# A two-layer decoder trunk on one Trainium2 core: both attentions' value projections by the seven-product form

## Chip, cores, metric

The program runs on one core of one Trainium2 chip. The metric is the device time of one execution in microseconds; the time before is the median of three runs.

A core has five engines that run side by side, each through its own list of instructions in a fixed order: PE (matmuls and transposes; PEld is its weight load), DVE (element by element arithmetic), ACT (copies, casts, activations), POOL, and SP, which here issues the weight loads. They wait for each other by semaphores. PE writes its sums to PSUM banks of 128 x 512 floats, from which DVE and ACT read.

## What is computed

Two layers; each is a token mixer, a cross-attention over 256 memory rows and a squared-ReLU MLP, all on 256 tokens of width 2048. The part that is changed is `v` below, in both layers:

```python
def memory_attention(h, mem_n, w_q, w_kv, w_o):
    q = (h @ w_q).reshape(bsz, seq, X_HEADS, X_HEAD_DIM)
    k, v = jnp.split(mem_n @ w_kv, 2, axis=-1)
    ...
    scores = jnp.einsum('bshd,bmhd->bhsm', q, k).astype(F32) * (X_HEAD_DIM ** -0.5)
    p = jax.nn.softmax(scores, axis=-1).astype(v.dtype)
    o = jnp.einsum('bhsm,bmhd->bshd', p, v).reshape(bsz, seq, X_HEADS * X_HEAD_DIM)
    return o @ w_o
```

`mem_n` is the memory after an RMS norm with a weight of its own in each layer; there are 4 heads of 512.

## The kernel before

**Precision.** Every float32 operand of a large product is split in two: `hi` is the value cast to fp32r by ACT, `lo` the rest, subtracted by DVE (`split`, L101 and L102). A product of 128 rows by 512 columns is then three matmuls: hi·hi, hi·lo, lo·hi. A weight tile of 256 rows by 512 columns (512 KB) is loaded by SP into `wraw` (4 buffers), split into `whi` and `wlo` (3 buffers each), and with two halves of the tokens, `t`, it feeds 12 matmuls. All operands of a layer's width lie in `act` tiles: 16 row tiles `kt`, hi and lo.

**An attention** (`attention`). `mem_prep` prepares the memory's rows in four pieces: POOL loads a chunk (`memc`, 2 buffers), and `scale_chunk` scales it by the norm's weight, hi on ACT (L232) and lo on DVE (L233). The pieces are side work: `tick`, called once for each weight tile, takes one and puts its instructions in with a lower priority. Then, head by head, `proj` makes q and k (`gemm_feat`, L163 and L165), and `softmax` the probabilities, transposed and split, `pTh` and `pTl`.

Then come the values, head by head: `gemm_tok` with `wv` (8 weight tiles, 96 matmuls, L145 to L147), the scaling by the row's norm into `vh` (ACT, L505) and `vl` (DVE, L506), 24 matmuls for the weighted sum over the memory's rows (L516, 256 columns each), and the split of that into `oT`. Head 0's output also goes through `token_sums`: four sums and differences of its row tiles and halves (L614 to L617) and their split, which the next product needs.

**The seven-product form** (`gemm_seven`). The output projection `wo` and most of the last MLP's down projection take two column tiles `n0` and `n0+1` at once. For the first four row tiles they form a 2 x 2 by 2 x 2 block product with seven products instead of eight: the left sums come from `token_sums`, the right ones are made from the four loaded weight tiles `ws` (L687, L693, L698, L703, into `run` or in place). Each product is a split and 6 matmuls; parts that belong to several outputs are copied out of PSUM by ACT (`kept`, L679) and added by DVE. The rest of the row tiles go the plain way (`direct`), between the products. At the end `gather` adds what is in the banks to the residual.

**Order.** The program is written in this order; a scheduler then lays each engine's list out, by priority and by its own estimate of when an operand is ready. Buffers come from pools with tags: tiles with one tag share its slots (2 in the attention's pool) and get them in the written order.

Of the kernel before, what the change touches and what calls it, by code (L numbers as in the profile page):

```python
# [16 lines left out]
P = 128  # L17
D = 2048
S = 256
# [19 lines left out]
class Trunk:  # L39
# [230 lines left out]
    def mem_prep(self, pool, layer):  # L270

        act = self.new_act()

        def piece(j):
            m = pool.tile([P, 4, S], F32, name="memc")
            self.nc.gpsimd.dma_start(out=m, in_=self.a["mem_t"][j])
            self.scale_chunk(m, 4 + layer, act, j)

        self.side += [lambda j=j: piece(j) for j in range(NCH)]
        return act  # L280


# [152 lines left out]
    def attention(self, x, layer, cur, nxt):  # L435
# [3 lines left out]
        with tc.tile_pool(name="at", bufs=2, reuse_waits="tile") as ap:  # L439
            qs = ap.tile([P, 2], F32, name="qs", bufs=1)  # L440
            nqs = ap.tile([P, 2], F32, name="nqs", bufs=1)
            pTs = []
            memT = self.mem_prep(ap, layer)

            def proj(act, w, n, nm):
                h = ap.tile([P, 4, S], F32R, name=nm + "h")
                l = ap.tile([P, 4, S], F32R, name=nm + "l")
                for i in range(2):
                    z = ap.tile([P, 2, S], F32, name="z")
                    self.gemm_feat(act, w, 2 * n + i, z)  # L450
                    self.split(h[:, 2 * i:2 * i + 2], l[:, 2 * i:2 * i + 2], z)
                return h, l

            def softmax(q, k, hd):
                sc = self.ps([P, 2, S])
                for t in range(2):
                    sl = slice(t * P, (t + 1) * P)
                    for f in range(4):
                        mm = lambda s, m, b, e: nc.tensor.matmul(  # L459
                            sc[:, t, :], s, m, start=b, stop=e, skip_group_check=True)  # L460
                        mm(q[0][:, f, sl], k[0][:, f, :], f == 0 and t == 0, False)
                        mm(q[0][:, f, sl], k[1][:, f, :], False, False)
# [12 lines left out]
                nc.vector.reciprocal(out=rs, in_=sm)  # L475
                for t in range(2):
                    nc.vector.tensor_scalar(out=e[:, t, :], in0=e[:, t, :], scalar1=rs[:, t:t + 1],
                                            scalar2=None, op0=ALU.mult)
                pt = self.ps([P, 2, S])
                for m in range(2):  # L480
                    for t in range(2):
                        nc.tensor.transpose(pt[:, m, t * P:(t + 1) * P], e[:, t, m * P:(m + 1) * P], self.ident)
                ph = ap.tile([P, 2, S], F32R, name="pTh", bufs=4)
                pl = ap.tile([P, 2, S], F32R, name="pTl", bufs=4)
                self.split(ph, pl, pt)
                pTs.append((ph, pl))

            for hd in range(HEADS):
                q = proj(hT, wq, hd, "q")
                self.flush()  # L490
                k = proj(memT, wk, hd, "k")
                if hd == 0:
                    rstd = cur.rstd()
                    nc.vector.tensor_scalar(out=qs, in0=rstd, scalar1=QSCALE, scalar2=None, op0=ALU.mult)
                    nc.vector.tensor_scalar(out=nqs, in0=rstd, scalar1=-QSCALE, scalar2=None, op0=ALU.mult)
                softmax(q, k, hd)

            oT = self.new_act()
            for hd in range(HEADS):
                acc = self.gemm_tok(memT, wv, hd)  # L500
                vh = ap.tile([P, 2, HD], F32R, name="vh")
                vl = ap.tile([P, 2, HD], F32R, name="vl")
                for t in range(2):
                    r = self.rstd_mem[:, t:t + 1]
                    nc.scalar.activation(out=vh[:, t, :], in_=acc[:, t, :], func=AF.Copy, scale=r)  # L505
                    nc.vector.scalar_tensor_tensor(out=vl[:, t, :], in0=acc[:, t, :], scalar=r,  # L506
                                                   in1=vh[:, t, :].bitcast(F32), op0=ALU.mult, op1=ALU.subtract)
                ph, pl = pTs[hd]
                ops = [self.ps([P, 2, S]) for _ in range(2)]
                for fp in range(2):  # L510
                    op = ops[fp]
                    for k in range(2):
                        f = 2 * fp + k
                        sl = slice(f * P, (f + 1) * P)
                        for m in range(2):
                            mm = lambda s, mv, b, e: nc.tensor.matmul(  # L516
                                op[:, k, :], s, mv, start=b, stop=e, skip_group_check=True)
                            mm(vh[:, m, sl], ph[:, m, :], k == 0 and m == 0, False)
                            mm(vh[:, m, sl], pl[:, m, :], False, False)
                            mm(vl[:, m, sl], ph[:, m, :], False, m == 1)  # L520
                    kt = 4 * hd + 2 * fp
                    self.split(oT[0][:, kt:kt + 2, :], oT[1][:, kt:kt + 2, :], op)
                if hd == 0:
                    for fp in range(2):
                        o = ap.tile([P, 2, S], F32, name="o", tag="e")
                        nc.scalar.copy(out=o, in_=ops[fp])
                        ops[fp] = o
                    sums = self.token_sums(ap.tile([P, KB * NB], F32, name="s", tag="qh"),
                                           lambda: ap.tile([P, 4, 2, P], F32R, name="sums", tag="kh"), *ops)

            nxt.start()
            count = iter(range(100))
            ws = lambda: ap.tile([P, KB * NB], F32, name="ws", tag=("ql", "qh")[next(count) % 2])
            run = lambda: ap.tile([P, KB * NB], F32, name="run", tag="kl")
            pair = {}

            def kept(i):
                if i in (1, 2):
                    return ap.tile([P, NB], F32, name="kept", tag="z")
                if i == 0:  # L540
                    pair[0] = ap.tile([P, 2, NB], F32, name="kept2", tag="kl")
                return pair[0][:, i // 3, :]

            def gather(t, n, part):
                xc = x[:, t, n * NB:(n + 1) * NB]
                nc.vector.tensor_tensor(out=xc, in0=part, in1=xc, op=ALU.add)

            for j in range(0, NCH, 2):
                self.gemm_seven((ws, run, kept), lambda kt, t: [f[:, kt, t * P:(t + 1) * P] for f in oT[:2]],
                                sums, wo, j, 0, gather)  # L550
                for n in (j, j + 1):
                    self.at(1 + n - j, lambda n=n: nxt.chunk(x, n))


    def mlp(self, x, layer, cur, nxt):
# [3 lines left out]
        with tc.tile_pool(name="ml", bufs=4, reuse_waits="tile") as mp:  # L559
# [5 lines left out]
            for b in range(DFF // D):  # L565
# [25 lines left out]
                for n in range(NCH):  # L591
                    end = b == DFF // D - 1
                    if nxt.closing and not (end and n >= NCH - 2):
                        if n % 2 == 0:
                            self.gemm_seven((ws, run, kept), lambda kt, t: [f[:, kt % 4, t * P:(t + 1) * P]
                                                                            for f in hid[kt // 4]],
                                            sums, wd, n, b * KT, gather)
                    elif nxt.closing and end and n == NCH - 1:
                        self.gemm_last(hid, wd, n, b * KT, lambda t, acc: (gather(t, n, acc), nxt.finish(x, t)))
                        break  # L600
# [18 lines left out]
        self.split(sh, sl, s)  # L619
        return sh, sl  # L620

    def gemm_seven(self, tiles, token, sums, w, n0, k0, gather):

# [90 lines left out]
        for keys in (((1, 0), (0, 1)), ((0, 0), (1, 1))):  # L714
            for e in ends:
                next(e)
            for t, j in keys:
                gather(t, n0 + j, banks[t, j])
        for e in ends:
            next(e, None)  # L720

# [648 lines left out]
```

## Time and profile before

| | us |
|---|---|
| median of 3 runs (2842.48 to 2843.86) | 2843.06 |
| the profiled execution, whole | 2844.99 |
| its span, first to last instruction | 2843.3 |

The profile is of one execution. Its page gives the busy time of each engine, the granted clock of PE (here 0.997 on the mean), the chain of work that ended last, and groups of instructions by line, engine, operation and tile. A timeline row is start, length, engine, line, operation, output and input; a bracket behind it is the idle time of the engine just ahead, and what ended it. Neighbouring instructions of one engine overlap a little: a matmul of 512 columns has a length of 0.39 us, though the next one begins earlier.

### The profile page before, as it was taken

What the parts mean: (1) busy time and instruction counts of PE and PEld (TensorE: products, weight loads), DVE (VectorE), ACT (ScalarE), POOL (GpSimd) and SP (SyncE); (2) the same over time, 40 slices, a digit from 0 to 9 for tenths busy, and PEclk for the clock granted to TensorE, in tenths of its full rate; (3) what the DMA queues carried; (4) which work ended last, traced back from release to release, by engine and by line L of the source; (5) the groups of instructions that cost most, each with busy time, mean ns of one, the idle gap of its engine ahead of it and who ended that gap; (6) DMA issues with size and microseconds to landing.
All of it is one profiled execution on the core that took longest, in us unless ns stands there. A gap on an engine that the chain in (4) does not pass through costs nothing.

```text
span 2843.3 us, 39689 instructions
## 1 busy us (share of the span) xinstructions
PE 2803.5 (99%) x15172; PEld 2347.3 (83%) x15172; DVE 1959.4 (69%) x2707; ACT 1394.7 (49%) x1801; POOL 204.8 (7%) x380
## 2 busy tenths in 40 slices
PE   8999999999999999999999999999999999999998
PEld 6888888888888888888787788888888888888886
DVE  6765655578878878787567666555677767667665
ACT  5445544454544444444455445444554545445453
POOL 1000000001022222222001000000000000000000
PEclk9999999999999999999999999999999999999999
DMA  8766665657677777776879766566556565565655
GB/s 282 212 202 207 194 179 185 183 163 230 191 221 219 218 224 222 216 223 207 231 240 296 220 203 209 181 182 195 166 181 213 166 217 188 167 218 162 223 159 155
DMA packets 180463, 579.55 MB, mean 204 GB/s; under 512 B 37440, under 2 KB 39664, under 8 KB 179504
## 3 DMA queue, kind: packets, MB, share of 16 engines
q1 hardware_dynamic: 141440, 511.77, 57.8%
q0 software_dynamic: 38688, 65.19, 8.5%
q8 instruction: 118, 1.93, 0.3%
q14 instruction: 73, 0.60, 0.1%
q10 hardware_dynamic: 144, 0.07, 0.0%
HBM read 553.88 MB, written 22.94 MB: 203 GB/s over the span
## 4 chain that ended last, share of the span: by engine, by line
PE 90%; DVE 4%; DMA 3%; ACT 1%; issue 1%; POOL 0%; SPq 0%; DVEq 0%; ACTq 0%; POOLq 0%
PE acc L163 24%; PE acc L650 15%; PE acc L165 13%; PE acc L146 7%; PE acc L147 7%; PE acc L145 7%; PE acc L735 4%; PE acc L734 4%; PE acc L733 4%; DVE wlo L102 1%; PE ps L516 1%; PE ps L459 1%; ACT whi L101 1%; PE ps L214 1%; DMA wraw<-in_f_w_down 1%
## 5 line engine op out<-in xcount | busy, mean ns | idle before, releaser
L102 DVE TENSOR_TENSOR wlo<-wraw,whi 128x1024 fp32r<-128x1024 f32 x908 | 1109.2, 1223 | 672.0 <-ACT whi L101 668.0
L101 ACT CAST whi<-wraw 128x1024 fp32r<-128x1024 f32 x908 | 954.9, 1052 | 1133.7 <-PE acc L163 374.4
L163 PE MATMUL acc<-act,whi 128*128 128x512 f32 x3072 | 1084.5, 397 | 0.5 <-ACT whi L101 0.4
L165 PE MATMUL acc<-act,wlo 128*128 128x256 f32 x3072 | 864.7, 281 | 1.3 <-DVE wlo L102 1.3
L163 PEld LDWEIGHTS acc<-act,whi 128*128 128x128 f32 x3072 | 576.3, 188 | 135.3 <-issue 1.6
L165 PEld LDWEIGHTS acc<-act,wlo 128*128 128x128 f32 x3072 | 580.2, 189 | 6.0 <-DVE wlo L102 2.2
L145 PE MATMUL acc<-whi,act 128*128 128x512 f32 x992 | 391.1, 394 | 8.7 <-ACT whi L101 7.3
L146 PE MATMUL acc<-wlo,act 128*128 128x512 f32 x992 | 389.2, 392 | 6.2 <-DVE wlo L102 6.2
L147 PE MATMUL acc<-whi,act 128*128 128x512 f32 x992 | 388.5, 392 | 0.3 <-DVE act L102 0.3
L145 PEld LDWEIGHTS acc<-whi,act 128*128 128x128 f32 x992 | 187.1, 189 | 49.4 <-ACT whi L101 8.6
L146 PEld LDWEIGHTS acc<-wlo,act 128*128 128x128 f32 x992 | 187.3, 189 | 46.1 <-DVE wlo L102 8.6
L147 PEld LDWEIGHTS acc<-whi,act 128*128 128x128 f32 x992 | 187.3, 189 | 38.6 <-DVE act L102 0.7
L734 PE MATMUL acc<-wlo,hh 128*128 128x512 f32 x544 | 215.5, 396 | 0.8 <-DVE wlo L102 0.8
L733 PE MATMUL acc<-whi,hh 128*128 128x512 f32 x544 | 215.1, 395 | 0.0
L735 PE MATMUL acc<-whi,hl 128*128 128x512 f32 x544 | 214.7, 395 | 0.0
L650 PE MATMUL acc<-wlo,hh 128*128 128x512 f32 x378 | 147.6, 390 | 1.6 <-DVE wlo L102 1.6
L650 PE MATMUL acc<-whi,hh 128*128 128x512 f32 x378 | 147.6, 391 | 0.5
L650 PE MATMUL acc<-whi,hl 128*128 128x512 f32 x378 | 147.2, 389 | 0.0
L650 PE MATMUL acc<-whi,act 128*128 128x512 f32 x432 | 135.8, 389 | 0.0
L734 PEld LDWEIGHTS acc<-wlo,hh 128*128 128x128 f32 x544 | 102.5, 188 | 24.5 <-DVE wlo L102 1.8
L735 PEld LDWEIGHTS acc<-whi,hl 128*128 128x128 f32 x544 | 102.5, 188 | 22.8 <-issue 1.6
L733 PEld LDWEIGHTS acc<-whi,hh 128*128 128x128 f32 x544 | 102.6, 189 | 22.5 <-issue 0.4
(325 smaller groups left out, 2726.1 us busy)
## 6 DMA issues: line engine op xcount, KB each, us to landing
wraw<-in_f_w_up SPq DMA_DIRECT2D x256, 512.0 KB, 4.2
wraw<-in_f_w_down SPq DMA_DIRECT2D x228, 512.0 KB, 4.3
wraw<-in_a_w_in SPq DMA_DIRECT2D x64, 512.0 KB, 4.4
wraw<-in_x_w_q SPq DMA_DIRECT2D x64, 512.0 KB, 3.7
wraw<-in_x_w_k SPq DMA_DIRECT2D x64, 512.0 KB, 3.7
wraw<-in_x_w_v SPq DMA_DIRECT2D x64, 512.0 KB, 3.6
wraw<-in_b_w_out SPq DMA_DIRECT2D x64, 512.0 KB, 4.5
wraw<-in_x_w_o SPq DMA_DIRECT2D x48, 512.0 KB, 3.8
```

What stands on the lines that cost most here:

```text
L101: self.nc.scalar.copy(out=hi, in_=src)
L102: self.nc.vector.tensor_tensor(out=lo, in0=src, in1=hi.bitcast(F32), op=ALU.subtract)
L145: nc.tensor.matmul(out[t], ah[:, kt, sl], hi[:, kk, :], start=st, stop=False)
L146: nc.tensor.matmul(out[t], ah[:, kt, sl], lo[:, kk, :], start=False, stop=False)
L147: nc.tensor.matmul(out[t], al[:, kt, sl], hi[:, kk, :], start=False, stop=en)
L163: nc.tensor.matmul(acc[:, f, :], hi[:, kk, sl], both[:, kt].rearrange("p a s -> p (a s)"), start=st, stop=False, skip_group_check=True)
L165: nc.tensor.matmul(acc[:, f, 0:S], lo[:, kk, sl], ah[:, kt, :], start=False, stop=en, skip_group_check=True)
L214: nc.tensor.transpose(pt[:, kk, t * P:(t + 1) * P], src[:, t, c:c + P], self.ident)
L650: mm = lambda s, m, e: nc.tensor.matmul(out, s, m, start=key not in begun, stop=e, skip_group_check=True)
L733: nc.tensor.matmul(acc[:, t, :], ah[:, kt % 4, sl], hi[:, kk, :], start=st, stop=False)
L734: nc.tensor.matmul(acc[:, t, :], ah[:, kt % 4, sl], lo[:, kk, :], start=False, stop=False)
L735: nc.tensor.matmul(acc[:, t, :], al[:, kt % 4, sl], hi[:, kk, :], start=False, stop=en)
```

## The change

The value projections also go through `gemm_seven`, two heads at a time. For that

- `mem_prep` takes the pieces in the order 1, 2, 3, 0, and piece 0 is scaled in place by four DVE instructions, split whole (one ACT cast, one DVE subtraction), and put through `token_sums` into `mem_sums`;
- `gemm_seven` takes a second function, `end`, for what is in the banks at its end. In `values` the parts are collected in `more`, added at the end where there is one, and scaled into `vh` and `vl`;
- the weighted sums of both heads (`weighted`) stand behind the pair's product, and head 0's `token_sums` behind its weighted sum, as before;
- the loaded tiles `ws` have a list of homes (slots of the v tiles for heads 0 and 1, then of the q tiles), `run` and `ends` have one fixed slot for the whole stage.

```diff
@@ mem_prep
-            self.scale_chunk(m, 4 + layer, act, j)
-
-        self.side += [lambda j=j: piece(j) for j in range(NCH)]
+            if j:
+                return self.scale_chunk(m, 4 + layer, act, j)
+            for k in range(4):
+                self.nc.vector.tensor_scalar(out=m[:, k, :], in0=m[:, k, :], scalar1=self.gcol[:, 4 + layer, k:k + 1],
+                                             scalar2=None, op0=ALU.mult)
+            self.split(act[0][:, 0:4, :], act[1][:, 0:4, :], m)
+            self.mem_sums = self.token_sums(pool.tile([P, KB * NB], F32, name="s", tag="vh"),
+                                            lambda: pool.tile([P, 4, 2, P], F32R, name="msums", tag="memc"),
+                                            m[:, 0:2], m[:, 2:4])
+
+        self.side += [lambda j=j: piece(j) for j in (1, 2, 3, 0)]
@@ attention
-            for hd in range(HEADS):
-                acc = self.gemm_tok(memT, wv, hd)
...
+            homes = iter(("vh", "vl") * 2 + ("ql", "qh") * 6)
+            ws = lambda: ap.tile([P, KB * NB], F32, name="ws", tag=next(homes))
+            run = ap.tile([P, KB * NB], F32, name="run", tag="kh")
+            ends = ap.tile([P, 2, NB], F32, name="ends", tag="kl")
+            kept = lambda i: ap.tile([P, NB], F32, name="kept", tag="z") if i in (1, 2) else ends[:, i // 3, :]
...
+                def end(t, n, src):
...
+                    part = more.pop((t, n), None)
+                    if part is not None:
+                        nc.vector.tensor_tensor(out=part, in0=src, in1=part, op=ALU.add)
+                        src = part
+                    vh, vl = (f[:, t, :] for f in vs[n - h0])
                     r = self.rstd_mem[:, t:t + 1]
+                    nc.scalar.activation(out=vh, in_=src, func=AF.Copy, scale=r)
+                    nc.vector.scalar_tensor_tensor(out=vl, in0=src, scalar=r, in1=vh.bitcast(F32),
+                                                   op0=ALU.mult, op1=ALU.subtract)
+
+                self.gemm_seven(tiles, token(memT), self.mem_sums, wv, h0, 0,
+                                lambda t, n, part: more.update({(t, n): part}), end)
+                return vs
...
+            for h0 in range(0, HEADS, 2):
+                vs = values(h0)
+                for i in range(2):
+                    ops = weighted(h0 + i, *vs[i])
+                    if h0 + i == 0:
...
+                        sums = self.token_sums(ap.tile([P, KB * NB], F32, name="s", tag="qh"),
+                                               lambda: ap.tile([P, 4, 2, P], F32R, name="sums", tag=next(tags)), *ops)
@@ gemm_seven
-                gather(t, n0 + j, banks[t, j])
+                end(t, n0 + j, banks[t, j])
```

Three places in the engines' lists, all laid out by the scheduler. Line numbers of the changed kernel are other than those of the profile: L675 is the matmul of `gemm_seven` (L650 before), L545 the weighted sum (L516), L529 `vl` (L506), L638 to L641 the sums (L614 to L617), L712 and L718 combinations of weight tiles.

**PE, end of head 0's values in layer 0.** Before; `acc` is head 1's product:

```order
L145 MATMUL acc_4304<-whi_4307,act_2322 128x512
L516 MATMUL ps_4261<-pTh_2827,vh_4255 128x256
L516 MATMUL ps_4261<-pTl_2828,vh_4255 128x256
L516 MATMUL ps_4262<-pTh_2827,vh_4255 128x256
L516 MATMUL ps_4262<-pTl_2828,vh_4255 128x256
L146 MATMUL acc_4304<-wlo_4308,act_2322 128x512
L516 MATMUL ps_4261<-pTh_2827,vl_4256 128x256
L516 MATMUL ps_4262<-pTh_2827,vl_4256 128x256
L147 MATMUL acc_4304<-whi_4307,act_2322 128x512
```

After, the last product of heads 0 and 1 and the first weighted sums (ps_4441 is head 0's, ps_4484 head 1's):

```order
L675 MATMUL acc_4120<-wlo_4405,act_2322 128x512
L675 MATMUL acc_4120<-whi_4404,act_2322 128x512
L545 MATMUL ps_4441<-pTh_2834,vh_4414 128x256
L545 MATMUL ps_4441<-pTl_2835,vh_4414 128x256
L545 MATMUL ps_4442<-pTh_2834,vh_4414 128x256
L545 MATMUL ps_4442<-pTl_2835,vh_4414 128x256
L545 MATMUL ps_4484<-pTh_3260,vh_4416 128x256
```

and the last of the 48 weighted sums and the first product of heads 2 and 3:

```order
L545 MATMUL ps_4485<-pTh_3260,vl_4417 128x256
L545 MATMUL ps_4485<-pTh_3260,vh_4416 128x256
L545 MATMUL ps_4485<-pTl_3261,vh_4416 128x256
L545 MATMUL ps_4485<-pTh_3260,vl_4417 128x256
L675 MATMUL acc_4514<-whi_4525,msums_2480 128x512
L675 MATMUL acc_4514<-wlo_4526,msums_2480 128x512
```

The next head's matmuls were mixed in among the weighted sums; now the 48 stand in one piece, with nothing of the next pair among them. In layer 1 the list is the same.

**DVE, the same place.** Before; `wlo` are head 1's weight splits, `act` is the split of `oT`, `s` and `sums` the row sums for wo:

```order
L102 TENSOR_TENSOR wlo_4326<-wraw_4323,whi_4325 128x1024
L506 SCALAR_TENSOR_TENSOR vl_4256<-acc_4110,rstd_mem_1959,vh_4255 128x512
L102 TENSOR_TENSOR wlo_4344<-wraw_4341,whi_4343 128x1024
L506 SCALAR_TENSOR_TENSOR vl_4256<-acc_4110,rstd_mem_1959,vh_4255 128x512
L102 TENSOR_TENSOR act_4109<-ps_4261,act_4109 128x2x256
L102 TENSOR_TENSOR act_4109<-ps_4262,act_4109 128x2x256
L102 TENSOR_TENSOR wlo_4362<-wraw_4359,whi_4361 128x1024
L614 TENSOR_TENSOR s_4295<-o_4291,o_4293 128x256
```

After, from the last `vl` on (ps_4485 is head 1's second half, `run` and `wlo_4526` the first right-hand sum of heads 2 and 3 and its split):

```order
L529 SCALAR_TENSOR_TENSOR vl_4417<-ends_4118,rstd_mem_1959,vh_4416 128x512
L102 TENSOR_TENSOR act_4116<-ps_4441,act_4116 128x2x256
L102 TENSOR_TENSOR act_4116<-ps_4442,act_4116 128x2x256
L640 TENSOR_TENSOR s_4475<-o_4471 128x256
L102 TENSOR_TENSOR act_4116<-ps_4484,act_4116 128x2x256
L638 TENSOR_TENSOR s_4475<-o_4471,o_4473 128x256
L102 TENSOR_TENSOR act_4116<-ps_4485,act_4116 128x2x256
L639 TENSOR_TENSOR s_4475<-s_4475,o_4471 128x256
L641 TENSOR_TENSOR s_4475<-o_4473,s_4475 128x256
L102 TENSOR_TENSOR sums_4481<-s_4475,sums_4480 128x1024
L712 TENSOR_TENSOR run_4117<-ws_4518,ws_4516 128x1024
L102 TENSOR_TENSOR wlo_4526<-run_4117,whi_4525 128x1024
```

The next product's splits stood ahead of the `oT` splits and the row sums; now they stand behind both.

**DVE, the last piece of the memory's rows in layer 1.** Before, the end of chunk 2, and chunk 3 around a weight split:

```order
L102 TENSOR_TENSOR wlo<-wraw,whi 128x1024
L233 SCALAR_TENSOR_TENSOR act<-memc,gcol,act 128x256 x4
L194 TENSOR_TENSOR rstd<-rstd,rstd_t_16223 128x2
L190 SCALAR_TENSOR_TENSOR rstd_t_16223<-rstd,rs_v 128x1
L102 TENSOR_TENSOR wlo<-wraw,whi 128x1024
L233 SCALAR_TENSOR_TENSOR act<-memc,gcol,act 128x256 x2
```

After, the end of chunk 3, and chunk 0:

```order
L233 SCALAR_TENSOR_TENSOR act<-memc,gcol,act 128x256 x2
L280 TENSOR_SCALAR memc<-memc,gcol 128x256 x4
L102 TENSOR_TENSOR wlo<-wraw,whi 128x1024
L638 TENSOR_TENSOR s<-memc 128x256
L102 TENSOR_TENSOR act<-memc,act 128x4x256
L639 TENSOR_TENSOR s<-s,memc 128x256
```

Chunk 0 stands where chunk 3 stood, its scalings ahead of a weight split, its low part behind that and one of the sums.

More of the change, by code (lines that the diff above doesn't have):

```diff
@@ L498, in attention, with values, weighted @@
             oT = self.new_act()
-            for hd in range(HEADS):
-                acc = self.gemm_tok(memT, wv, hd)
-                vh = ap.tile([P, 2, HD], F32R, name="vh")
-                vl = ap.tile([P, 2, HD], F32R, name="vl")
-                for t in range(2):
-                    r = self.rstd_mem[:, t:t + 1]
-                    nc.scalar.activation(out=vh[:, t, :], in_=acc[:, t, :], func=AF.Copy, scale=r)
-                    nc.vector.scalar_tensor_tensor(out=vl[:, t, :], in0=acc[:, t, :], scalar=r,
-                                                   in1=vh[:, t, :].bitcast(F32), op0=ALU.mult, op1=ALU.subtract)
+            homes = iter(("vh", "vl") * 2 + ("ql", "qh") * 6)
[3 more added lines that the diff above has]
+            kept = lambda i: ap.tile([P, NB], F32, name="kept", tag="z") if i in (1, 2) else ends[:, i // 3, :]
+            tiles = ws, lambda: run, kept
+            token = lambda act: lambda kt, t: [f[:, kt, t * P:(t + 1) * P] for f in act[:2]]
+            def values(h0):
+                vs, more = [], {}
+                def end(t, n, src):
+                    if not vs:
+                        vs.extend([ap.tile([P, 2, HD], F32R, name=nm) for nm in ("vh", "vl")] for _ in range(2))
+                    part = more.pop((t, n), None)
[3 more added lines that the diff above has]
+                    vh, vl = (f[:, t, :] for f in vs[n - h0])
+                    r = self.rstd_mem[:, t:t + 1]
+                    nc.scalar.activation(out=vh, in_=src, func=AF.Copy, scale=r)
[4 more added lines that the diff above has]
+                return vs
+            def weighted(hd, vh, vl):
                 ph, pl = pTs[hd]
@@ L522, in attention @@
                     self.split(oT[0][:, kt:kt + 2, :], oT[1][:, kt:kt + 2, :], op)
[L523 to L529, printed above, removed]
-            nxt.start()
[L532 to L542, printed above, removed]
+                return ops
+            for h0 in range(0, HEADS, 2):
[3 more added lines that the diff above has]
+                    if h0 + i == 0:
+                        for fp in range(2):
+                            o = ap.tile([P, 2, S], F32, name="o", tag="e")
+                            nc.scalar.copy(out=o, in_=ops[fp])
+                            ops[fp] = o
+                        tags = iter(("kh", "kl"))
+                        sums = self.token_sums(ap.tile([P, KB * NB], F32, name="s", tag="qh"),
+                                               lambda: ap.tile([P, 4, 2, P], F32R, name="sums", tag=next(tags)), *ops)
+            nxt.start()
             def gather(t, n, part):
@@ L548, in attention @@
             for j in range(0, NCH, 2):
-                self.gemm_seven((ws, run, kept), lambda kt, t: [f[:, kt, t * P:(t + 1) * P] for f in oT[:2]],
-                                sums, wo, j, 0, gather)
+                self.gemm_seven(tiles, token(oT), sums, wo, j, 0, gather, gather)
                 for n in (j, j + 1):
@@ L596, in mlp @@
                                                                             for f in hid[kt // 4]],
-                                            sums, wd, n, b * KT, gather)
+                                            sums, wd, n, b * KT, gather, gather)
                     elif nxt.closing and end and n == NCH - 1:
@@ L620, in token_sums, with gemm_seven @@
         return sh, sl
-    def gemm_seven(self, tiles, token, sums, w, n0, k0, gather):
+    def gemm_seven(self, tiles, token, sums, w, n0, k0, gather, end):
         nc = self.nc
```

## The prediction

> **What bounds the kernel now.** I read the page from the top: first the busy shares, then the chain of work that ended last, then the waits.
>
> ```profile
> PE 2803.5 (99%) x15172; PEld 2347.3 (83%) x15172; DVE 1959.4 (69%) x2707; ACT 1394.7 (49%) x1801; POOL 204.8 (7%) x380
> PE 90%; DVE 4%; DMA 3%; ACT 1%; issue 1%; POOL 0%; SPq 0%; DVEq 0%; ACTq 0%; POOLq 0%
> ```
>
> PE is busy for 2803.5 of 2843.3 us, so it stands idle for only about 40 us in the whole program, and 90% of the last chain is PE. A matmul less is time saved, and any wait of PE is time lost: nothing later has slack in which it could be won back. Two stretches, layer 0's value projection from a little ahead to a little behind, and a stretch of layer 1's, with the columns PE, PEld, DVE, ACT, POOL, granted clock, DMA share and GB/s:
>
> ```profile
> 467.00:660.00 193.00, 193.00 (x932) 161.06 (x932) 126.70 (x151) 96.20 (x115) 6.07 (x16) 1.00 0.58 178
> 2000.00:2200.00 200.00, 200.00 (x1013) 168.89 (x1012) 138.97 (x164) 105.66 (x137) 2.14 (x4) 1.00 0.60 189
> ```
>
> There PE has no idle time at all, DVE is busy 66% and ACT 50%. So on the sum of work there is room for more on DVE and ACT; whether it is there at the right moment is a question of order. The pitch of the matmuls comes from the timeline of PE:
>
> ```profile
> 1993.51 0.39 PE L145 MATMUL acc<-whi,act 128*128 128x512 f32 x1
> ...
> 1998.95 0.39 PE L145 MATMUL acc<-whi,act 128*128 128x512 f32 x1
> ...
> 2010.31 0.28 PE L516 MATMUL ps<-pTl,vh 128*128 128x256 f32 x1
> 2010.43 0.28 PE L516 MATMUL ps<-pTh,vh 128*128 128x256 f32 x1
> ```
>
> Between the first two lie 24 matmuls of the value projection: 5.44 us, **0.227 us each**; its 0.39 us is a length, of which 0.16 overlaps the next. The weighted sums (L516, 256 columns) go every 0.12 us.
>
> **What it removes.** Each pair of heads has 7 products instead of 8 for the first four row tiles: 6 matmuls less, 24 in the two layers. 24 x 0.227 = **5.4 us**, and this is all that there is to gain.
>
> **What it adds in sum.** For each pair of heads DVE gets three weight splits, four combinations of weight tiles, three additions to kept parts and one sum of kept parts; ACT three splits and four copies. By the rows below that is 7 x 1.22 + 4 x 0.68 = 11.3 us of DVE a pair, 23 a layer: 126.7 + 23 = 150 of 193 us in the first stretch. ACT gets 3 x 1.05 + 4 x 0.59 = 5.5 a pair. By sums this lies beside PE and I cost it at nothing; the weight loads stay 64 of 512 KB. What it costs where the cover is gone are the next two parts.
>
> **The end of heads 0 and 1, in both layers.** Durations (busy sum and mean ns; the last row is a load, us to landing):
>
> ```profile
> L102 DVE TENSOR_TENSOR wlo<-wraw,whi 128x1024 fp32r<-128x1024 f32 x908 | 1109.2, 1223 | 672.0 <-ACT whi L101 668.0 <-PE ps L992 0.2
> L546 DVE TENSOR_TENSOR x<-acc,x 128x512 f32<-128x512 f32 x16 | 10.3, 682 | 0.4 <-PE acc L650 0.4
> L687 DVE TENSOR_TENSOR run<-ws 128x1024 f32<-128x1024 f32 x11 | 13.4, 1221 | 0.1
> L102 DVE TENSOR_TENSOR act<-ps,act 128x512 fp32r<-128x512 f32 x32 | 21.3, 688 | 13.7 <-ACT act L101 12.4
> L102 DVE TENSOR_TENSOR sums<-s,sums 128x1024 fp32r<-128x1024 f32 x2 | 2.5, 1225 | 0.0
> L617 DVE TENSOR_TENSOR s<-o,s 128x256 f32<-128x256 f32 x2 | 0.8, 424 | 0.1
> L679 ACT COPY kept<-acc 128x512 f32<-128x512 f32 x44 | 24.8, 589 | 8.1 <-PE acc L650 8.1
> L505 ACT ACTIVATE vh<-acc,rstd_mem 128x512 fp32r<-128x512 f32 x16 | 11.0, 690 | 13.3 <-PE acc L147 13.3
> L101 ACT CAST act<-ps 128x512 fp32r<-128x512 f32 x32 | 17.9, 586 | 20.0 <-PE ps L516 20.0
> L101 ACT CAST sums<-s 128x1024 fp32r<-128x1024 f32 x2 | 2.1, 1055 | 0.4 <-DVE s L617 0.4
> L101 ACT CAST whi<-run 128x1024 fp32r<-128x1024 f32 x33 | 34.8, 1055 | 29.2 <-PE acc L650 14.5 <-issue 6.1 <-PE acc L163 5.2
> wraw<-in_x_w_v SPq DMA_DIRECT2D x64, 512.0 KB, 3.6
> ```
>
> Before, the order on PE lets the next head's matmuls run between the weighted sums, with their weight splits on DVE ahead of the sums of rows. After, PE has all 48 weighted sums of heads 0 and 1 directly behind the first pair's last product, and the second pair's first product directly behind those; DVE has the first split of the second pair behind the oT splits and behind the sums for wo, which wait for the weighted sums. So the cover is gone on both sides. With T for the moment at which PE could issue on:
>
> - Ahead of the weighted sums: the last product lands at T+0.16, the part is added (0.68), ACT makes vh (0.69): PE goes on at about T+1.6. **Wait 1.6.**
> - Weighted sums: 48 x 0.12 = 5.8, issued by T+7.35, landed at T+7.5. Then in a row: ACT casts the last of oT (0.59), DVE its low part (0.69), two sums (2 x 0.42), ACT casts the sums (1.06), DVE their low part (1.22), the first combination (1.22, beginning some 0.1 early, as neighbours on DVE do), ACT its cast (1.06). With some 0.04 for each of the handovers that is T+14.2; PE has been free since T+7.35. **Wait 6.9.**
> - The second matmul needs the low part (1.22), one matmul of 0.23 lies beside it. **Wait 1.0.**
> - DVE is now at its start with five operations ahead of the next direct tile (two splits, two combinations, its own split; 1.14 apart): 15.4 + 5 x 1.14 = T+21.1, while PE has 17 matmuls, held by their own two splits, and is through at T+19.5. **Wait 1.5.** Later tiles have 12 matmuls (2.7 us) against one or two operations, so it gets back its lead.
>
> Sum 11.0 a layer, **22.0** in both. At the end of heads 2 and 3 the order on PE puts 13 matmuls of wo (3.0 us) ahead of the weighted sums, over the 1.6, and wo goes on behind them with splits that are made: 0, at most the same 1.6 a layer. SP's order: the second loaded tile of the second pair (its slot of tag qh comes behind that of the sums) goes out behind the first pair's last raw tiles; 3.6 us from issue to landing, long before T+12. The fourth waits for the sums' low part (T+12.0), lands at about T+15.6 and is first read by the third of those five operations, at T+17.7: 2 us of slack. Behind it SP holds wo's tiles and the raw tiles from the fifth on; four raw tiles are in the buffers. I cost SP at nothing; a load of double length (3.6 more) would make it 1.6 a layer.
>
> **The rows of the memory.** Chunk 0, which k's first matmul reads, is now prepared last of the four, and in more steps. Layer 1, from the timelines of ACT, DVE and PE, and the price of the new scaling (its nearest row, a scaling by a column):
>
> ```profile
> 1766.29 0.91 ACT L232 ACTIVATE act<-memc,gcol 128x256 fp32r<-128x256 f32 x2 [2.81 <-DMA memc<-in_mem_t]
> 1769.32 0.87 DVE L233 SCALAR_TENSOR_TENSOR act<-memc,gcol,act 128x256 fp32r<-128x256 f32 x2
> 1766.71 0.40 PE L163 MATMUL acc<-act,whi 128*128 128x512 f32 x1
> L477 DVE TENSOR_SCALAR e<-e,rsm 128x256 f32<-128x256 f32 x16 | 4.9, 351 | 0.3
> ```
>
> The fourth piece lands at 1766.25 (ACT stood 2.81 us for it) and is ready at 1770.2. Before, this was chunk 3, the last that k reads; k begins at 1766.71, with chunk 0. Now: four scalings 1.15 us (0.27 apart), to 1767.4; ACT's cast to 1768.5, beside it a weight split and one sum on DVE, to 1768.9; low part (1.22) to 1770.1. PE begins k at about 1770.2: **3.5 us.** Bounds: 3.0, if nothing lay between cast and low part, and 4.7, if the scalings had the 0.44 of the row above each and two more sums went ahead. The sums themselves are needed much later: nothing. Layer 0:
>
> ```profile
> 310.36 1.67 DVE L233 SCALAR_TENSOR_TENSOR act<-memc,gcol,act 128x256 fp32r<-128x256 f32 x4
> 314.90 0.39 PE L163 MATMUL acc<-act,whi 128*128 128x512 f32 x1
> ```
>
> There the piece is in its buffer when DVE comes to it at 310.36: scalings to 311.5, a sum and a split to 313.0, low part to 314.2, ahead of 314.90. Nothing, with 0.7 us to spare.
>
> **The clock after a wait.** One wait of this length is in the trace, between two stages; then the matmuls behind it, and the window's granted clock (the last number but two):
>
> ```profile
> 1383.77 0.33 PE L214 MATMUL ps<-ident,x 128*128 128x128 f32 x1 [2.73 <-DVE x L588]
> ...
> 1386.18 0.63 PE L734 MATMUL acc<-wlo,hh 128*128 128x512 f32 x1
> ...
> 1387.89 0.51 PE L735 MATMUL acc<-whi,hl 128*128 128x512 f32 x1
> 1384.70:1388.10 3.40, 3.40 (x13) 0.50 0.95 368
> ```
>
> After 2.73 us (and 0.33 more) PE ran 3.4 us at half the clock: 4 matmuls in 1.71 us, 0.43 each. That takes 3.4 x (1 - 0.227/0.43) = 1.6 us. So I add 1.6 behind the wait of 3.5. Behind the wait of 6.9 the same is sure to come, but there PE loses 1.0 and 1.5 to DVE anyway, and a slower PE lets DVE catch up: 0.3 a layer, 0.6, between nothing and two such windows (3.2 a layer).
>
> [...]
>
> **Sum.** -5.4 + 22.0 + 0.6 + 3.5 + 1.6 = **+22.3 us**. On the profiled execution (2844.99 us for the span of 2843.3) that is 2867.3; it ran 1.9 above the median, which gives 2843.06 + 22.3 = **2865.4**.
>
> **Rivals.**
>
> - *The stalls are covered.* The matmuls go, and PE finds its splits made, as it does in both stretches above (no idle time). Then -5.4: 2837.6, and not slower. Its mechanism is a DVE that has the second pair's first split done by T+7.35; the price is nothing, and it decides from waits under 2.7 us a layer. For it speaks that DVE has 43 us free in the stretch; against it that the free time lies elsewhere, since each engine keeps its order and the split stands behind the sums. 4 in 100. Since 0.2% (5.7 us, about what a measurement of this kernel can tell from no change) is more than 5.4, even this is no clear gain.
> - *The memory rows are in time.* If the last piece lands 3.5 us sooner, -5.4 + 22.0 + 0.6: 2860.3. For it: the piece of layer 0 was there in time. Against: its load starts when the second piece's buffer is free, as before. 20 in 100.
> - *The clock costs its full price.* Two windows behind each long wait: -5.4 + 22.0 + 6.4 + 3.5 + 3.2 = +29.7, 2872.8. [...] Against: the work behind it waits for DVE anyway. 17 in 100.
> - *It doesn't do what it says*: excluded, the order of PE has 24 matmuls less.
>
> **How the numbers follow.** My forecast, with some us on either side, has 55 in 100; 4 are left for what I don't see (a late load, splits that lag for longer). Faster by over 0.2%: 1 in 100; within 0.2%: 4, the first rival; slower: 95. The range goes from 2856 (the second rival, with 1.5 + 1.5 us less should DVE's last lag be covered in both layers and the clock cost nothing) to 2874 (the third, and a little of SP's 1.6).
>
> **What would show it.** Right: PE waits of 6 to 8 us in both layers, released by ACT at the cast of a combination (whi from run), behind the weighted sums of heads 0 and 1; PE idle at the first weighted sum for some 1.6; PE idle for about 3.5 at k's first matmul in layer 1 and not in layer 0; windows at clock 0.50 behind these. Busy PE time without them falls by some 5 us. Wrong: no such wait in the list of PE's waits, or the splits of the second pair on DVE ahead of the sums; then the first rival holds. If PE waits there for a DMA, my reading of SP is wrong.

## The result and the profile after

The changed kernel takes **2866.42 us** in the median of 5 runs (2864.29 to 2869.78), the kernel before 2842.58 us (2842.48 to 2843.86): a ratio over the rounds of **1.0087, 95% interval 1.0076 to 1.0098** (the two medians alone give 1.0084). The forecast was 2865.4, in a range of 2856 to 2874. The profiled execution took 2864.42 us, with a span of 2862.7 us, 19.4 more than the span before.

First the busy shares and the chain that ended last, on the page of the changed kernel:

```profile
PE 2804.2 (98%) x15148; PEld 2348.5 (82%) x15148; DVE 2003.9 (70%) x2763; ACT 1417.3 (50%) x1825; POOL 204.7 (7%) x380
PE 88%; DVE 5%; DMA 3%; ACT 2%; issue 2%; POOL 0%; SPq 0%; DVEq 0%; ACTq 0%; POOLq 0%
```

PE has 24 matmuls less (15148 against 15172) and is still busy for 0.7 us more. That is a first hint of the clock, since the same matmul is busy for longer at half of it (0.80 us where 0.39 is usual, below). The list of PE's waits (us in total, times, longest) says where the rest went:

```profile
PE acc L675 <- ACT whi L101: 13.6, 2, 6.8
...
PE ps L545 <- ACT vh L528: 3.1, 2, 1.5
PE acc L675 <- DVE wlo L102: 3.1, 6, 0.5
...
PE acc L163 <- DVE act L102: 2.7, 1, 2.7
```

None of the first, second and fourth stood in the list before. There are two long waits, one for each layer, released by ACT's cast; two short ones ahead of the weighted sums (L545); and one at k's first matmul (L163), which is in layer 1 alone. On the timeline the shorter two are these, the first in layer 0:

```profile
527.51 0.39 PE L545 MATMUL ps<-pTh,vh 128*128 128x256 f32 x1 [1.54 <-ACT vh L528]
...
1777.43 0.47 PE L163 MATMUL acc<-act,whi 128*128 128x512 f32 x1 [2.74 <-DVE act L102]
```

The chain behind the long wait in layer 0 is on the timeline of DVE, from the last of the oT splits on:

```profile
534.08 0.69 DVE L102 TENSOR_TENSOR act<-ps,act 128x512 fp32r<-128x512 f32 x1
534.69 0.41 DVE L639 TENSOR_TENSOR s<-s,o 128x256 f32<-128x256 f32 x1
535.14 0.42 DVE L641 TENSOR_TENSOR s<-o,s 128x256 f32<-128x256 f32 x1
536.67 1.22 DVE L102 TENSOR_TENSOR sums<-s,sums 128x1024 fp32r<-128x1024 f32 x1 [1.11 <-ACT sums L101]
537.82 1.22 DVE L712 TENSOR_TENSOR run<-ws 128x1024 f32<-128x1024 f32 x1
540.20 1.22 DVE L102 TENSOR_TENSOR wlo<-run,whi 128x1024 fp32r<-128x1024 f32 x1 [1.16 <-ACT whi L101]
```

and PE beside it, with the last weighted sum of head 1 and the first product of heads 2 and 3:

```profile
533.15 0.28 PE L545 MATMUL ps<-pTh,vl 128*128 128x256 f32 x1
...
540.22 0.80 PE L675 MATMUL acc<-whi,msums 128*128 128x512 f32 x1 [6.79 <-ACT whi L101]
```

From one start to the other it is 7.07 us, of which 0.12 is the matmul's own pitch: 6.95 for the step that the forecast put at 6.9. The sequence on DVE is the one that was predicted, operation by operation. That matmul took 0.80 us where 0.39 is usual, because the granted clock was 0.50 there (first stretch below). Three stretches (columns PE, PEld, DVE, ACT, POOL, granted clock, DMA share, GB/s), behind the long wait of layer 0, behind that of layer 1, and behind k's:

```profile
535.90:546.10 10.20, 5.42 (x12) 3.95 (x13) 8.26 (x8) 4.72 (x5) 0.00 (x0) 0.50 0.35 103
2003.70:2010.50 6.80, 3.61 (x8) 2.53 (x9) 5.63 (x6) 3.22 (x4) 0.00 (x0) 0.50 0.41 97
1778.40:1781.80 3.40, 3.40 (x12) 2.81 (x11) 3.36 (x5) 1.57 (x2) 0.00 (x0) 0.50 0.26 70
```

Half clock lasted 10.2, 6.8 and 3.4 us there: three windows of 3.4 us, two, and one. Part of the first two stretches lies inside the wait itself, where it costs nothing: PE's first product came only at 540.22 in layer 0 and at 2006.42 in layer 1. PE worked for 5.42 and 3.61 us at half clock there. By the two pitches of the forecast, 0.227 and 0.43 us, that is an estimated 2.6 and 1.7 us lost.

### The profile page after: what moved, and what is told of

Its sections match the earlier page's. It is cut to its first block, busy times and chain, and to the rows that moved or that the text cites. A ratio compares the mean times of both kernels' runs of the same rounds, so it can differ in the third digit from the quotient of the medians.

```text
span 2862.7 us, 39726 instructions
## 1 busy us (share of the span) xinstructions
PE 2804.2 (98%) x15148; PEld 2348.5 (82%) x15148; DVE 2003.9 (70%) x2763; ACT 1417.3 (50%) x1825; POOL 204.7 (7%) x380
## 4 chain that ended last, share of the span: by engine, by line
PE 88%; DVE 5%; DMA 3%; ACT 2%; issue 2%; POOL 0%; SPq 0%; DVEq 0%; ACTq 0%; POOLq 0%
PE acc L163 24%; PE acc L675 20%; PE acc L165 12%; PE acc L146 5%; PE acc L145 5%; PE acc L147 5%; PE acc L760 4%; PE acc L759 4%; PE acc L758 4%; DVE wlo L102 2%; ACT whi L101 1%; PE ps L467 1%; DMA wraw<-in_f_w_down 1%; PE ps L545 1%; PE ps L214 1%
## 5 line engine op out<-in xcount | busy, mean ns | idle before, releaser
L102 DVE TENSOR_TENSOR wlo<-wraw,whi 128x1024 fp32r<-128x1024 f32 x892 | 1088.9, 1222 | 643.7 <-ACT whi L101 639.7
L101 ACT CAST whi<-wraw 128x1024 fp32r<-128x1024 f32 x892 | 938.5, 1052 | 1116.7 <-PE acc L163 371.4
L163 PE MATMUL acc<-act,whi 128*128 128x512 f32 x3072 | 1083.9, 396 | 3.3 <-DVE act L102 2.7
L163 PEld LDWEIGHTS acc<-act,whi 128*128 128x128 f32 x3072 | 576.7, 188 | 136.7 <-issue 4.6
L145 PE MATMUL acc<-whi,act 128*128 128x512 f32 x736 | 291.9, 397 | 9.9 <-ACT whi L101 8.4
L146 PE MATMUL acc<-wlo,act 128*128 128x512 f32 x736 | 290.3, 394 | 3.5 <-DVE wlo L102 3.5
L147 PE MATMUL acc<-whi,act 128*128 128x512 f32 x736 | 288.9, 392 | 0.3 <-DVE act L102 0.3
L675 PE MATMUL acc<-whi,act 128*128 128x512 f32 x864 | 273.7, 391 | 0.6 <-DVE ends L524 0.5
L675 PEld LDWEIGHTS acc<-whi,act 128*128 128x128 f32 x864 | 162.9, 189 | 36.1 <-ACT whi L101 1.3
L145 PEld LDWEIGHTS acc<-whi,act 128*128 128x128 f32 x736 | 139.6, 190 | 40.8 <-ACT whi L101 8.8
L675 PE MATMUL acc<-wlo,act 128*128 128x512 f32 x432 | 169.7, 393 | 0.6 <-DVE wlo L102 0.5
L146 PEld LDWEIGHTS acc<-wlo,act 128*128 128x128 f32 x736 | 139.7, 190 | 34.0 <-DVE wlo L102 6.1
L147 PEld LDWEIGHTS acc<-whi,act 128*128 128x128 f32 x736 | 139.5, 190 | 29.6 <-DVE act L102 0.7
L675 PE MATMUL acc<-wlo,hh 128*128 128x512 f32 x378 | 147.6, 391 | 1.6 <-DVE wlo L102 1.6
L675 PE MATMUL acc<-whi,hh 128*128 128x512 f32 x378 | 147.6, 390 | 0.5
L675 PE MATMUL acc<-whi,hl 128*128 128x512 f32 x378 | 147.1, 389 | 0.0
```

The costliest lines, as they stand in the source:

```text
L101: self.nc.scalar.copy(out=hi, in_=src)
L102: self.nc.vector.tensor_tensor(out=lo, in0=src, in1=hi.bitcast(F32), op=ALU.subtract)
L145: nc.tensor.matmul(out[t], ah[:, kt, sl], hi[:, kk, :], start=st, stop=False)
L146: nc.tensor.matmul(out[t], ah[:, kt, sl], lo[:, kk, :], start=False, stop=False)
L147: nc.tensor.matmul(out[t], al[:, kt, sl], hi[:, kk, :], start=False, stop=en)
L163: nc.tensor.matmul(acc[:, f, :], hi[:, kk, sl], both[:, kt].rearrange("p a s -> p (a s)"), start=st, stop=False, skip_group_check=True)
```

## The experiments

The theory: the time goes to the **order** at the end of heads 0 and 1 (weighted sums, then row sums, then the second pair's first split, each in its place on an engine that keeps its order), and to chunk 0 of the memory, prepared last. Its rival: the seven-product form is simply **too much work** for DVE and ACT beside PE, and the waits are where that shows first. e1 to e4 tell these apart; the last three measure what the clock costs. Each ratio is against the kernel before on the same chip in the same rounds.

| kernel | median us | ratio to before, 95% interval |
|---|---|---|
| changed kernel | 2866.42 | 1.0087 (1.0076 to 1.0098) |
| e1, row sums later | 2840.18 | 0.9998 (0.9989 to 1.0007) |
| e2, other buffers | 2855.50 | 1.0053 (1.0040 to 1.0067) |
| e3, k's order | 2860.56 | 1.0066 (1.0054 to 1.0079) |
| e4, e1 and e3 together | 2836.20 | 0.9980 (0.9971 to 0.9989) |
| e5, changed kernel again | 2867.15 | 1.0090 (1.0076 to 1.0103) |
| e6, spare matmuls at the boundary | 2860.28 | 1.0066 (1.0054 to 1.0079) |
| e7, the same, and ahead of k | 2859.88 | 1.0062 (1.0051 to 1.0074) |

### e1: the row sums later

```diff
-                        tags = iter(("kh", "kl"))
-                        sums = self.token_sums(ap.tile([P, KB * NB], F32, name="s", tag="qh"),
-                                               lambda: ap.tile([P, 4, 2, P], F32R, name="sums", tag=next(tags)), *ops)
+                        self.at(6, lambda ops=ops: sums.extend(row_sums(ops)))
```

`row_sums` holds the removed call; `at(6, ...)` makes it six direct tiles into the second pair. In this kernel's order of PE, 13 matmuls of the second pair stand ahead of the weighted sums.

> Head 0's row sums for wo are made six direct tiles into the second pair instead of right behind its weighted sums; nothing else is changed, and no work is added or taken away. Theory (order: the second pair's first split stands on DVE behind the sums, and these behind the weighted sums): 13 matmuls of the second pair come ahead of the weighted sums, and the waits of 1.9, 7.1 and 1.3 us at the boundary are gone in both layers, each to under 0.3, with no window below clock 1.00 there. Left is -5.4 for the matmuls and the wait at k in layer 1 (2.7 to 3.0, and 1.6 of half clock): 2842.6 - 5.4 + 4.5 = 2841.7 (2840 to 2844). Rival (load: 23 us more of DVE in a layer don't fit beside PE wherever they stand): PE waits for the low parts of the weights in the second pair, 3 us a layer or more, and the time is above 2850.

The waits of the boundary are gone in both layers but for 0.26 us, where the last of those 13 matmuls waits for DVE to read a PSUM bank, with the same number of instructions on PE, DVE and ACT. The stretch from 500 to 560 us of this kernel:

```profile
500.00:560.00 60.00, 59.74 (x286) 49.84 (x285) 45.18 (x48) 33.73 (x40) 0.00 (x0) 1.00 0.58 172
```

PE is busy for 59.74 of 60 us at full clock, and DVE for 45.18. And this is the order on DVE that makes it possible:

```profile
521.89 1.23 DVE L102 TENSOR_TENSOR wlo<-run,whi 128x1024 fp32r<-128x1024 f32 x1 [1.49 <-ACT whi L101]
...
524.30 0.74 DVE L529 SCALAR_TENSOR_TENSOR vl<-acc,rstd_mem,vh 128x512 fp32r<-128x512 f32 x1
```

The second pair's first low part (wlo from run) is now made ahead of the first pair's low parts of the values. Left in the list of waits is `L163 <- DVE act`, at k, with 2.6. So the rival falls for the boundary: the same work fits beside PE, and what it cost was its place. Moving the call also changes when the scratch of the row sums takes its slot of `qh`; e1 alone doesn't tell the two apart. In time the kernel comes out even with before (0.9998), in the range expected.

### e2: only the buffers of four tiles

```diff
-            homes = iter(("vh", "vl") * 2 + ("ql", "qh") * 6)
+            homes = iter(("vh", "vl") * 2 + ("ql", "ql", "qh", "qh") * 3)
```

> One line is changed: the second pair's four loaded tiles take the buffers ql, ql, qh, qh instead of ql, qh, ql, qh, so that the first two, of which the first combination is made, don't come behind the scratch of the row sums in qh. Everything else is as in the changed kernel, the row sums too. Theory (order): the first two products (12 matmuls, 2.7 us) go ahead of the weighted sums; the wait ahead of these is gone, and the long wait moves to the third product, whose split still stands behind the sums: 7.1 less the combination and the low part that are no longer in the chain, 4 to 5 us, then some 2.5 in small ones. That is some 5 us a layer less than the changed kernel: 2866.4 - 10 = 2856 (2851 to 2861). Rival 1 (load of DVE): the waits stay in sum, 2864 or more. Rival 2 (the load of the tile that came behind the sums held PE up): no waits are left, 2842.

The waits of PE in layer 0 at the boundary:

```profile
528.04 0.39 PE L545 MATMUL ps<-pTh,vh 128*128 128x256 f32 x1 [0.33 <-ACT vh L528]
537.71 0.79 PE L675 MATMUL acc<-whi,act 128*128 128x512 f32 x1 [3.75 <-ACT whi L101]
```

The wait ahead of the weighted sums is down from 1.54 to 0.33, and the long one went from the first product (operands whi and msums) to the third (whi and act), with 3.75 instead of 6.79; 4 to 5 had been expected, so it was a little shorter. The time, 2855.50, lies where the theory put it (2856), between the two rivals. Row sums and all else are as in the changed kernel. So one line that names four buffers moves 10 us: with other slots the first two products stand ahead of the row sums, which themselves have not moved. By what rule the scheduler draws the order from this was not tried.

### e3: k in the order in which its rows are made

```diff
-        for kc in range(KT // FK):
+        for i in range(KT // FK):
+            kc = (i + k0) % (KT // FK)
```

with `k0 = 1` for k and 0 for all else, and the first and last matmul of a group counted by `i`.

> k's projections go over the memory's chunks in the order 1, 2, 3, 0, in which they are prepared, instead of 0, 1, 2, 3; the rest is as in the changed kernel. Theory (in layer 1 k waits for chunk 0 alone, which is now prepared last): the wait of 2.7 us (3.0 idle) at k's first matmul and the half clock behind it are gone, chunk 0 is read only 8 us later; layer 0 has no wait there before and none now; the boundary's waits stay: 2866.4 - 3.0 - 1.6 = 2861.8 (2860.5 to 2863.5). Rival (the memory's preparation as a whole is late in layer 1, by its loads or by the added work on DVE): PE waits at the second to fourth chunk instead, and the time stays within 1.5 us of 2866.4.

The wait is gone, and only one of 0.28 us, for a weight's low part, is left behind it; the stretch around k's beginning in layer 1:

```profile
1765.00:1785.00 20.00, 19.73 (x111) 16.82 (x111) 17.52 (x34) 11.84 (x16) 0.53 (x1) 1.00 0.74 236
```

Clock 1.00, and 0.27 us of idle time in 20. The boundary's waits (13.6 in two) are those of the changed kernel. Expected was 4.6 us less than this, measured (1.0087 - 1.0066) x 2842 = 6.0, with intervals that overlap a little. The traces are narrower: from q's first matmul in layer 1 to q's first of head 1 it is 46.9 us before, 51.0 in the changed kernel and 47.2 here. The rival, a preparation that is late as a whole, is out.

### e4: both

> The edits of the two kernels with later row sums and with k's order in one. Theory: both waits are gone, nothing else has been added to PE, and the 24 matmuls show: 2842.6 - 5.4 = 2837.2 (2835.5 to 2839), faster than both kernels. Rival (the seven-product form costs PE something beside these waits, by small waits for splits in both pairs or by loads): above 2840, with waits of PE at the added products that before doesn't have.

2836.20 us, in the range expected; 0.9980 is 5.7 us less than before (3.1 to 8.2 by the interval), which the forecast's -5.4 for the 24 matmuls would explain alone. In the trace, from the last matmul of k's projections to the first of the MLP, it is 2.6 and 2.2 us less than before in the two layers. This version is the fastest of all kernels here. Small waits are left: the 0.26 us of e1, and in layer 1 one of 1.12 us for a weight split of k, behind DVE, which had stood 1.50 us for chunk 0's load. From q's first matmul there to q's first of head 1 it is 48.3 us in this execution, against 46.9 before.

### e5, e6, e7: what the clock costs

e5 is the changed kernel as it stands. e6 fills the long wait with matmuls that nobody reads (the computation is not changed by it), e7 also k's wait in layer 1:

```diff
+                if h0 == 0:
+                    spare = self.ps([P, 2 * S])
+                    for _ in range(28):
+                        nc.tensor.matmul(spare, pTs[1][0][:, 0, 0:P], pTs[1][0].rearrange("p m s -> p (m s)"),
+                                         start=True, stop=True, skip_group_check=True)
```

> The changed kernel once more, as it is, beside the two kernels below on the same chip. Both theories: 1.0087 of before (1.0076 to 1.0098), the same waits at the boundary (1.5 to 1.9, 6.8 to 7.1, 1.3 us) and at k in layer 1 (2.6 to 4.7 us, by the runs so far), with two or three half-clock windows behind each long wait.

> The changed kernel with 28 matmuls of 512 columns more in each layer, whose result nobody reads, between the last weighted sum of head 1 and the second pair's first product: 28 x 0.227 = 6.4 us of the 6.8 in which PE stands there. Both theories: no half-clock window at the boundary; the first product begins when its split is there, as before. Theory 1 (as in the prediction: the slower PE only waits less for DVE): the waits for DVE behind it come back, 1.0 for the first low part and 1.5 at the next direct tile, and the time falls by 0.6 to 3 us from the changed kernel's. Theory 2 (a half-clock window costs its 1.6 us whole): five windows gone, 8 us less than the changed kernel.

> As the kernel with 28 spare matmuls at the boundary, and 11 more (2.5 us) ahead of k's first matmul in layer 1, where PE stands 2.6 us or more. Theory: the wait there is one for DVE and doesn't change, the window of half clock behind it is gone, and with it 1.6 us against the kernel with spare matmuls at the boundary alone. Rival: the clock behind this wait costs nothing (k waits for splits there anyway), the same time within 0.5 us.

In e5 the waits at the boundary are the expected ones, 1.54 and 6.8 us in both layers. k's wait, 5.35, lies outside the 2.6 to 4.7 that were expected. The same 28 us around the boundary of layer 0, first of the changed kernel, then of e6:

```profile
532.00:560.00 28.00, 20.74 (x86) 16.56 (x84) 22.02 (x24) 16.27 (x20) 0.00 (x0) 0.82 0.42 132
```

```profile
532.00:560.00 28.00, 26.80 (x126) 21.68 (x125) 23.72 (x26) 17.74 (x22) 0.00 (x0) 1.00 0.47 139
```

With e6 the clock is whole, and PE's first product begins when its split is there, as before:

```profile
541.20 0.49 PE L680 MATMUL acc<-whi,msums 128*128 128x512 f32 x1 [0.43 <-ACT whi L101]
542.46 0.51 PE L680 MATMUL acc<-wlo,msums 128*128 128x512 f32 x1 [0.77 <-DVE wlo L102]
```

From the last weighted sum of head 1 to the first of head 2 it is 54.2 us in both layers, against 56.9 and 55.7 in the changed kernel and 56.2 and 56.1 in e5: 2.0 us a layer on the mean, in both layers 4.0. The time fell by more, 2867.15 - 2860.28 = 6.9, but the intervals of the two ratios touch, so the traces say it more narrowly. Theory 1 had 0.6 to 3, theory 2 had 8: **the truth lies between**. It is not the clock alone, either: in e6 one combination of weight tiles came to stand behind the direct tile's split on DVE instead of ahead of it (1.14 us), which takes away most of the wait of 1.5 that the forecast had there (estimated from the rows of e6, 1.2 us would have come). That a kernel with full clock and the old order would lose this 1.5 was not tried.

At k the effect stands alone, in one execution of each. The stretch from 1771 to 1785 us of e6, then of e7:

```profile
1771.00:1785.00 14.00, 10.34 (x47) 8.67 (x46) 10.79 (x23) 6.14 (x7) 0.00 (x0) 0.76 0.65 198
```

```profile
1771.00:1785.00 14.00, 12.69 (x68) 10.60 (x68) 12.17 (x27) 6.62 (x8) 0.00 (x0) 1.00 0.69 212
```

From k's first matmul in layer 1 to q's first of head 1 it is 23.3 us before, 25.7 in e6 and 23.4 in e7: the half clock behind k's wait cost 2.4 us there and costs 0.1 with PE kept busy. The way to k's first matmul is the same (27.4 and 27.5 us from q's first, 23.5 before). Over whole runs the 0.4 us between e6 and e7 tells nothing, since each varies by more.

## Why the prediction was right

By its own steps, the mechanism as the runs showed it, and two sizes that were off:

- **The gain of 5.4.** Right within the noise: e4 has -5.7 (-3.1 to -8.2), and 4.8 less in the traces of its two value stages with wo.
- **Added work costs nothing in sum.** Right: in e1 and e4 DVE has 2763 operations as in the changed kernel, and no wait of PE at the boundary is over 0.26 us.
- **Ahead of the weighted sums, 1.6.** Measured 1.54, in both layers.
- **First product of the second pair, 6.9.** Measured 6.95 in both layers. That the row sums and their place make it was shown by moving them (e1) and by moving the buffers (e2).
- **Its low part, 1.0.** In e6, at full clock, the second matmul starts 1.26 us behind the first, 1.03 more than the pitch of 0.227. In the changed kernel the half clock hides part of it.
- **The next direct tile, 1.5, and the clock, 0.3 a layer.** The step that was mis-sized. The wait did not appear: at half clock PE was so slow that DVE had caught up. In layer 0 the tile's low part was ready at 547.10 (the first row below, start and length), and PE came to it at 548.08; in layer 1 it was ready 0.1 us ahead of PE.

```profile
545.88 1.22 DVE L102 TENSOR_TENSOR wlo<-wraw,whi 128x1024 fp32r<-128x1024 f32 x1
...
548.08 0.39 PE L675 MATMUL acc<-wlo,act 128*128 128x512 f32 x1
```

  In its place stands the clock. Together, from the last matmul of k's projections to the first of the MLP, layer 0 takes 10.6 us more than before and layer 1 8.9 (in e5 9.2 in each); with the 2.7 that the layer saves these are 13.3, 11.6, 11.9 and 11.9, on the mean **12.2 where the forecast had 11.3**. The forecast gave the clock 0.3 because "a slower PE lets DVE catch up": right in kind, but half clock cost more than that lag.
- **End of heads 2 and 3: 0.** Right, but for 0.26 us at the 13th matmul of wo, less than the 1.6 that was left open.
- **SP at nothing.** Right for the splits ahead of the second pair's first products, which waited for no load. But 20 us later a loaded tile of wo was late: DVE stood 0.80 us for it in layer 0 and 0.39 in layer 1, and PE 0.52 and 0.11 us for the weight split behind it (0.66 and 0.56 in e5). The kernel before has no wait of PE there.

```profile
558.38 1.23 DVE L712 TENSOR_TENSOR run<-ws 128x1024 f32<-128x1024 f32 x1 [0.80 <-DMA ws<-in_x_w_o]
559.53 1.22 DVE L102 TENSOR_TENSOR wlo<-wraw,whi 128x1024 fp32r<-128x1024 f32 x1
```

```profile
560.80 0.50 PE L675 MATMUL acc<-wlo,act 128*128 128x512 f32 x1 [0.52 <-DVE wlo L102]
```

- **k in layer 1, 3.5, none in layer 0.** Right in place: layer 0 has the same 23.1 us from q's first matmul to k's in both kernels. The chain is as long as predicted: from the first scaling to k's first matmul 3.89 us, where the forecast had 3.95 (1766.25 to 1770.2).

```profile
1773.54 1.14 DVE L280 TENSOR_SCALAR memc<-memc,gcol 128x256 f32<-128x256 f32 x4
...
1776.07 1.22 DVE L102 TENSOR_TENSOR act<-memc,act 128x1024 fp32r<-128x1024 f32 x1
```

  How much of it PE feels depends on when the pieces land and when DVE comes to them: the forecast began the chain at the landing, as it is in e6 (DVE stands 1.19 us for it), but in the execution above the scalings came directly behind the third piece's low part. The five executions with this order of k have k's first matmul 2.9 (changed kernel), 2.7 (e1), 4.9 (e2), 5.5 (e5) and 3.8 us (e6) later than before, 4.0 on the mean, and behind it the clock took 1.0 to 2.8 where 1.6 stood in the sum. 5.1 was forecast for the two; the five have 5.7 on the mean.
- **The rivals.** "The stalls are covered" is out for this order, and true for that of e1. "The memory rows are in time" did not come about: k was late in layer 1 in all five executions. "The clock costs its full price" was right that two or three windows come, but not on the price: part of them lay inside the wait, and an estimated 2.6 and 1.7 us were lost where it had 3.2.

That the single forecast fell 1.0 us from the median is luck in part: the boundary cost 0.9 us a layer more than forecast and k 0.6, while executions of one kernel here differ by 4 to 11 us in all sets but the first of the kernel before (1.4). The profiled one, at 2864.42, has 4.2 us less than the terms measured in it (13.3 + 11.6 for the boundaries, 4.1 for k, -5.4) add up to; these came back where the change does nothing: 1.7 ahead of q's first matmul in layer 0, 1.1 in the stages between the layers, 1.4 in the last MLP.

## What to carry to other kernels

Where two stages share rolling buffers, look at what holds the buffer ahead of the next stage's first operand: a scratch of a late result there can put the whole next stage behind it, on engines that have time enough. A saving of 5 us in matmuls is lost with one seam of 7 us in each layer, so give PE independent work across each seam, or move what is not urgent (here the row sums) behind it. And read a chunk in the order in which it is made ready: k's rotation adds no work, and took away k's first wait; in e4 1.1 us of it came back at a later split.

## What the chip showed unexpectedly

**Half clock after a shorter gap than the forecast's 2.73 us.** The same gap of PE stands in the kernel before and in e1, in the stage between the layers, 1.44 and then 0.27 us; before, then e1:

```profile
1553.01 0.50 PE L145 MATMUL acc<-whi,act 128*128 128x512 f32 x1 [1.44 <-ACT act L101]
...
1554.01 0.50 PE L147 MATMUL acc<-whi,act 128*128 128x512 f32 x1 [0.27 <-DVE act L102]
```

```profile
1544.46 0.50 PE L145 MATMUL acc<-whi,act 128*128 128x512 f32 x1 [1.44 <-ACT act L101]
...
1545.46 0.50 PE L147 MATMUL acc<-whi,act 128*128 128x512 f32 x1 [0.27 <-DVE act L102]
```

In the kernel before, the clock behind it stayed at 1.00; in e1 it was 0.50 for the next 3.4 us. In the traces of before and of the changed kernel, all 18 changes of the granted clock lie on a grid of 3.41 us, to within 0.01; a window is one step of it. On that grid, before's gap is cut in two (1.27 and 0.32 us of idle time by the rows), e1's lies in one window (1.63; each row with the window behind it):

```profile
1552.00:1555.30 3.30, 2.03 (x8) 1.38 (x9) 3.02 (x7) 3.21 (x9) 0.00 (x0) 1.00 1.05 274
1555.40:1558.70 3.30, 2.98 (x18) 2.31 (x17) 1.98 (x3) 3.21 (x8) 0.00 (x0) 1.00 1.03 281
```

```profile
1543.10:1546.50 3.40, 1.77 (x6) 1.16 (x7) 3.13 (x6) 3.30 (x10) 0.00 (x0) 1.00 1.05 261
1546.60:1549.90 3.30, 3.30 (x11) 2.51 (x10) 1.67 (x3) 2.32 (x6) 0.00 (x0) 0.50 1.02 236
```

I laid that grid over the nine profiled executions, without the first 40 and the last 20 us, and counted the full-clock windows with over 0.5 us of idle PE time: of 103 with up to 1.53 us none was followed by half clock, of 19 with 1.83 or more all were, and of 18 between these 6 were. In before and the changed kernel alone, the longest idle time with no half clock behind it is 1.81 us (changed kernel, window from 1495.05), the shortest with it 1.79 (1525.77). So in these executions the border is between 1.53 and 1.83 us, about half a window; this is a count, no experiment made for it.

It may explain a part of why executions of one kernel differ: whether a gap of 1.4 to 3 us falls into one window or is cut in two can change from one to the next, and each window more costs an estimated 1.6 us at most, by the forecast's two pitches. That is not shown, and not the whole: beside e1 to e4 the kernel before spread over 11 us at mean clocks of 0.996 to 0.998, a difference of some three windows (each takes an estimated 0.0006 off the mean, 3.41 x 0.50 / 2843), or an estimated 5 us. In e4, whose longest gap behind the start is 1.79 us, the trace shows no such window between its beginning and its end.

**A second window follows while PE waits at half clock.** With the waits of 6.8 us came two windows in five of six cases and three in one. The same count for the windows at half clock is clear-cut: of 35, the 25 with up to 0.53 us of idle PE time were followed by full clock, and the 10 with 0.67 or more by another window at 0.50, as the one with 1.37 us in layer 0 of the changed kernel.
